# Inverting three head pairs beside the first scan of a RWKV-7 / Mamba-2 / MoE block instead of one

## The chip, the cores and the metric

The kernel runs on one core of a Trainium2 chip. The metric is device time in microseconds of one execution; lower is better. A core has five engines with a queue each: TensorE (PE in the rows; PEld is its weight load), VectorE (DVE), ScalarE (ACT), GpSimd (POOL) and SyncE (SP), whose queue here issues most of the transfers.

## What is computed

The reference is one layer of a backbone: a mixer of two parallel branches (bidirectional RWKV-7 and bidirectional Mamba-2), merged by gates, and then a mixture of experts, over 512 latent and 256 context tokens of width 1024. The change lies in the RWKV-7 branch, whose core is this recurrence, run forwards and backwards for 16 heads of 64:

```python
def step(s, inp):
    r_t, w_t, k_t, v_t, kk_t, a_t = inp
    sa = jnp.einsum('bhvk,bhk->bhv', s, -kk_t)
    s = s * w_t[:, :, None, :] + sa[..., None] * (kk_t * a_t)[:, :, None, :] + v_t[..., None] * k_t[:, :, None, :]
    return s, jnp.einsum('bhvk,bhk->bhv', s, r_t)
```

## The kernel before

**The chunked form.** The kernel cuts the 768 tokens into 12 chunks of 64 and works on pairs of heads, 0 to 7. Within a chunk the recurrence is a triangular system, so each chunk needs the inverse of a 64x64 unit triangular matrix. With 12 chunks, two heads and two directions, that is 48 matrices for each pair.

**The preparation.** `rw_all` goes through the eight pairs. For each it makes the decay products (`rw_elem`) and the masked products of a chunk (`rw_products`), once for each direction, and stores them in HBM: the 32x32 diagonal blocks go to `d1`, the off-diagonal block to `d3`. After the second direction it runs the pair's inverse, `tri`.

**The inverse, first step.** `tri` (L768 to L810) loads the blocks of `d1` into `Ad` with three transfers, works out the inverses of the 32x32 blocks on VectorE (L783 to L805), turns them on ScalarE (L808) and stores them and their transposes in `d2`. It is a generator with 16 resumptions: eight in the loop of L783 and L784, four in that of L795 and L797, four in that of L803 and L805. All pairs share the tiles `T` and `Tf`, so the inverses run one after the other.

**The inverse, second step.** `tri2` (L812 to L853) loads two pieces from `d2` and `d3` with eight transfers, waits `LAG` resumptions (if called with the tag "A"), multiplies them on TensorE in four groups of 48 small matmuls (`px`, L835, and `py`, L845) with a copy by ScalarE after each, and stores the full 64x64 inverses in `TTd` for the scan. It has `LAG` + 5 resumptions with that tag. In the preparation the second step of pairs 0 to 4 runs two pairs later, within `rw_products`.

**The scan.** `scan` does the 12 chunk steps of two pairs at once, so there are four scans. A step has three hand-overs on TensorE: `pr` (the right side, L901) is copied to `R` by VectorE (L929); `pq` = inverse times `R` is copied into `SV`, half by VectorE (L943) and half by ScalarE (L944); `pn`, the new state, is multiplied by the decay on VectorE (L953). Between the hand-overs `feed(HOP)`, with `HOP` = 3200, puts columns of the input projection (L311, L314) on TensorE: the filler, 24 blocks with a convolution behind each on VectorE and ScalarE (L464, L467), together with two late parts of the modulation, which it draws in between. The filler has about as many columns as the four scans ask for. A block needs its weights split in two (`whi` L283 on ScalarE, `wlo` L286 on VectorE).

**The side work.** Scan 0 also resumes a generator five times in each step (once after `R`, once after `pq`, three times, `SS`, at the end), 60 times in all; it is `rw_last`, with `LAG` = 9. It lets four resumptions pass, then runs the second step of pair 5, the first step of pair 7, and the second steps of pairs 6 and 7. What is left of it runs after scan 0, with `feed(SF)` after each resumption and `SF` = 2000. Scan 1 needs none of the results of pairs 5 to 7; scan 2 needs pair 5's, scan 3 those of pairs 6 and 7. After scan 3 the readout of the last two pairs (`rw_out`) runs alone, and the gate projections and the SSD stage follow.

**What sets the order.** In these stages only TensorE keeps the written order (`manual_schedule(engines={PE})`). The queues of VectorE, ScalarE, GpSimd and SyncE are put in order ahead of time by a planner, which works with costs of its own and prefers what was written earlier among the operations that are ready.

Of the kernel before, what the change touches and what calls it, by code (L numbers as in the profile page):

```python
# [35 lines left out]
ORB = 1  # L36
N1 = 15000
N2 = 11000
LAG = 9
R0 = 3000  # L40
SF = 2000
HE = 0, 1
SS = 3
RA = 0
PL = (0, 1, -1, -2, 2, 3, 4, 5, 6, 7)
PO = (0, 1, 2, 3, 4, 5, 6, 7, 8, 9)
FH = 2
# [39 lines left out]
class Block:  # L87
# [468 lines left out]
    def rw_all(self, pool, ps, z):  # L556

        self.fill, self.credit = self.rw_in(pool, z), 0
        next(self.fill)
        hop = R0  # L560
        f = lambda x=1: self.feed(x * (hop if len(self.kvr) < 8 else RHT))
        self.pair = {}
        self.drain(0)
        self.rw_head(pool, ps, 0, f)
        op = self.rw_elem(pool, ps, 0, 0, f)
        t2 = iter(())
        for p in range(8):
            nxt = self.rw_elem(pool, ps, p, 1, f)
            hop = RHOP
            self.rw_products(pool, ps, p, 0, *op, f, t2)  # L570
            op = nxt
            if 1 < p < 7:
                t2 = self.tri2(self.tp, ps, "ra", p - 2)
                next(t2)
            if p < 7:
                self.drain(p + 1)
            self.rw_bonus(pool, ps, p)
            if p < 7:
                self.rw_head(pool, ps, p + 1, f)
                nxt = self.rw_elem(pool, ps, p + 1, 0, f)  # L580
            self.rw_products(pool, ps, p, 1, *op, f, t2, p == 7)
            op = nxt
            if p < 7:
                self.finish(self.tri(self.tp, p))
        self.feed(1 << 30)

    def rw_last(self, ps):

        for _ in range(4):
            yield  # L590
        yield from self.tri2(self.tp, ps, "A", 5)
        yield from self.tri(self.tp, 7)
        yield from self.tri2(self.tp, ps, "A", 6)
        yield from self.tri2(self.tp, ps, "A", 7)

    def two(self, ps):
        return ps.tile([128, SEQ], F32, name="ra", tag="ra"), ps.tile([128, CTX], F32, name="rac", tag="ra")
# [214 lines left out]
    def tri2(self, pool, ps, tag, p):  # L812
# [12 lines left out]
        for d in range(2):  # L825
            nc.sync.dma_start(A21[64 * d:64 * d + 32], d3[d])
        for _ in range(LAG if tag == "A" else 1):
            yield
# [65 lines left out]
    def scan(self, pool, ps, p, side):  # L894
# [10 lines left out]
        for s in range(12):  # L905
# [19 lines left out]
            R = pool.tile([128, 2, 2, 64], F32, name="R", tag="R", bufs=2)  # L925
            if p == 0 and s < RA:
                nc.scalar.activation(R, pr, AF.Copy)
# [1026 lines left out]
def body(tc, A, out):  # L1954
    with ExitStack() as ctx:
# [28 lines left out]
        with ExitStack() as hx:  # L1984
# [22 lines left out]
            with pl("ip", space=PSUM) as B.ip, pl("sc") as sc, pl("scp", space=PSUM) as scp, ExitStack() as scx:  # L2007
# [5 lines left out]
                with tc.manual_schedule(engines={mybir.EngineType.PE}):  # L2013
                    for p in range(4):
                        py = B.scan(sc, scp, p, side)
                        if p == 0:
                            for _ in side:
                                B.feed(SF)
                            tpx.close()
# [96 lines left out]
```

## Time and profile before

| | us |
|---|---|
| median of three runs | 2141.14 |
| lowest and highest | 2135.18, 2143.14 |
| profiled execution, its own time | 2138.47 |
| its span, first to last instruction | 2136.7 |
| mean granted TensorE clock (share of full speed) | 0.933 |

The profile records one execution. The preparation runs until about 623 us, scan 0 from there to about 758, the scans 1 to 3 to about 1102. A row of a timeline gives the start, the duration, the engine and the line, what was written from what, and how often; in square brackets stands the time for which the engine idled before it, if any, and what released it. `pch` is the psum tile of all three hand-overs of a scan, so its rows are told apart by their inputs: `SV,sAL` makes the right side, `R,sTT` the value, `SV,sBT` the new state. In the first two steps the inputs have other names (`sAR`, `sBK`), as they lie in buffers of the preparation.

### The profile page before, as it was taken

The numbers are of one execution on the slowest core, as the hardware profiler recorded it, in microseconds if no ns is written. First come the engines' busy times: TensorE is split into PE (matmuls) and PEld (weight loads), VectorE is DVE, ScalarE is ACT, GpSimd is POOL, SyncE is SP. The second block draws the span as 40 slices with busy tenths as digits, with TensorE's granted clock in tenths as the row PEclk, the third lists the DMA queues.
The fourth block names the chain that finished last, engine by engine and source line by source line (L and its number), as shares of the span: only waits on it lengthen the run. The fifth ranks groups of instructions, "written<-read, shape, count | busy, mean of one in ns | idle before, by whom it ended". The sixth has DMA issues, their size and how long they took to land.

```text
span 2136.7 us, 34532 instructions
## 1 busy us (share of the span) xinstructions
PE 1880.0 (88%) x13683; PEld 1255.7 (59%) x13696; DVE 1244.5 (58%) x2234; ACT 840.0 (39%) x1344; POOL 259.2 (12%) x383
## 2 busy tenths in 40 slices
PE   5978898888869988999998997799999999999997
PEld 2867676676646756667675664377877453433332
DVE  4466988897888567555654898864364022322224
ACT  5454565545624343443543453353233131111113
POOL 1123323133220000000000000000001000000002
PEclk8999989999979989999998998889999999999998
DMA  6357687777888766785536353358567989999997
GB/s 239 89 128 179 161 201 181 177 175 184 206 199 241 229 225 217 257 254 157 180 102 203 121 170 104 108 180 287 187 247 292 355 333 362 409 409 409 409 409 292
DMA packets 388414, 495.13 MB, mean 232 GB/s; under 512 B 138521, under 2 KB 278031, under 8 KB 385179
## 3 DMA queue, kind: packets, MB, share of 16 engines
q1 hardware_dynamic: 349883, 407.33, 57.4%
q0 software_dynamic: 21504, 68.70, 11.0%
q10 hardware_dynamic: 16864, 16.88, 2.5%
q8 instruction: 108, 1.77, 0.3%
q14 instruction: 55, 0.45, 0.1%
HBM read 393.96 MB, written 97.98 MB: 230 GB/s over the span
## 4 chain that ended last, share of the span: by engine, by line
PE 53%; DVE 18%; DMA 13%; ACT 8%; issue 6%; POOL 1%; SPq 1%; ACTq 0%; POOLq 0%; DVEq 0%
PE ph L1712 9%; PE pl L311 9%; DMA wraw<-in_w_in_dram 5%; PE pye L1799 5%; PE pch L901 4%; PE mp L1361 4%; PE pc L314 3%; DVE wlo L286 2%; DMA ew<-in_exp_w_dram 2%; PE psc L1822 1%; PE sps L1180 1%; ACT whi L283 1%; PE py L901 1%; PE pl L1314 1%; PE adaps L167 1%
## 5 line engine op out<-in xcount | busy, mean ns | idle before, releaser
L311 PE MATMUL pl<-hlH,whi 128*128 128x512 f32 x672 | 244.1, 443 | 14.2 <-ACT u L455 5.6
L311 PE MATMUL pl<-hlH,wlo 128*128 128x512 f32 x672 | 236.3, 428 | 0.0
L311 PE MATMUL pl<-hlL,whi 128*128 128x512 f32 x672 | 231.9, 425 | 0.0
L1713 PE MATMUL ph<-ew,xe 128*64 128x512 f32 x432 | 196.3, 597 | 2.1 <-DMA ew<-in_exp_w_dram 2.1
L1712 PE MATMUL ph<-ew,xe 128*64 128x512 f32 x432 | 196.0, 596 | 0.0
L283 ACT ACTIVATE whi<-wraw 128x1024 fp32r<-128x1024 f32 x93 | 97.8, 1052 | 182.2 <-DMA wraw<-in_w_in_dram 79.1
L311 PEld LDWEIGHTS pl<-hlH,whi 128*128 128x128 f32 x672 | 132.8, 202 | 56.7 <-issue 14.1
L286 DVE TENSOR_TENSOR wlo<-wraw,whi 128x1024 fp32r<-128x1024 f32 x93 | 112.8, 1212 | 84.1 <-ACT whi L283 58.7
L311 PEld LDWEIGHTS pl<-hlL,whi 128*128 128x128 f32 x672 | 129.3, 196 | 38.1 <-issue 11.4
L311 PEld LDWEIGHTS pl<-hlH,wlo 128*128 128x128 f32 x672 | 128.3, 196 | 36.6 <-issue 12.6
L1712 PEld LDWEIGHTS ph<-ew,xe 128*64 128x64 f32 x432 | 56.3, 137 | 105.9 <-issue 104.5
L1799 PE MATMUL pye<-ew,ewx 128*64 128x512 f32 x448 | 108.3, 635 | 0.0
L314 PE MATMUL pc<-hcH,whi 128*128 128x256 f32 (+1 forms) x312 | 97.2, 315 | 7.1 <-ACT u L455 6.1
L464 DVE SCALAR_TENSOR_TENSOR cacc<-u,cst,cacc 128x772 f32<-128x772 f32 (+1 forms) x96 | 93.3, 972 | 11.1 <-ACT cacc L460 9.6
L314 PE MATMUL pc<-hcL,whi 128*128 128x256 f32 (+1 forms) x312 | 94.6, 307 | 0.0
L314 PE MATMUL pc<-hcH,wlo 128*128 128x256 f32 (+1 forms) x312 | 94.4, 304 | 0.0
L1719 ACT ACTIVATE ewx<-ph 128x512 f32<-128x512 f32 x30 | 17.9, 598 | 187.2 <-PE ph L1713 170.0
L1827 DVE TENSOR_TENSOR macc<-macc,psc 128x512 f32<-128x512 f32 x56 | 37.7, 685 | 91.4 <-PE psc L1822 91.3
L314 PEld LDWEIGHTS pc<-hcH,whi 128*128 128x128 f32 (+1 forms) x312 | 63.0, 202 | 15.8 <-ACT u L455 9.2
L1799 PEld LDWEIGHTS pye<-ew,ewx 128*64 128x64 f32 x448 | 32.7, 146 | 63.8 <-issue 63.1
L1815 DVE TENSOR_TENSOR yhl<-yf,yhl 64x512 fp32r<-64x512 f32 x30 | 20.5, 686 | 81.0 <-ACT yhl L1814 80.5
L1217 ACT ACTIVATE X<-selb,ncumT 128x128 f32<-128x128 f32 x128 | 36.4, 367 | 78.4 <-PE selb L1214 78.3
(594 smaller groups left out, 4100.4 us busy)
## 6 DMA issues: line engine op xcount, KB each, us to landing
ew<-in_exp_w_dram SPq DMA_DIRECT2D x126, 1024.0 KB
ew<-in_exp_w_dram SPq DMA_DIRECT2D x90, 512.0 KB
wraw<-in_w_in_dram SPq DMA_DIRECT2D x83, 512.0 KB
adaw<-in_ada_w_dram SPq DMA_DIRECT2D x24, 1024.0 KB
cst<-in_exp_w_dram SPq DMA_DIRECT2D x14, 1024.0 KB
BTd<-BT ACTq DMA_DIRECT2D x48, 256.0 KB
sAL<-ALd SPq DMA_DIRECT2D x23, 512.0 KB
sBT<-BTd SPq DMA_DIRECT2D x23, 512.0 KB
```

The costliest lines, as they stand in the source:

```text
L283: pin(nc.scalar.activation(hi, raw, AF.Copy))
L286: self.lo.tensor_sub(lo, raw, hi.bitcast(F32))
L311: nc.tensor.matmul(pl[:n], w_[:, kt, :n], x[0][:, kt, :], **e)
L314: nc.tensor.matmul(pc[:n], w_[:, kt, :n], x[1][:, kt, :], **e)
L464: e.scalar_tensor_tensor(acc[:, s0:s0 + n0], u[:, s0 + k:s0 + k + n0], cw[:, b, k:k + 1], acc[:, s0:s0 + n0], op0=OP.mult, op1=OP.add)
L901: mm = lambda o, w, x, f=True, l=True: nc.tensor.matmul(o, w, x, start=f, stop=l, skip_group_check=True)
L1217: nc.scalar.activation(X[:, c], pt[d][:, c], AF.Identity, bias=self.ncumT[:, c, r:r + 1])
L1361: nc.tensor.matmul(po[ob], w[k][lo][:, ob * 128:ob * 128 + 128], yb[k][:, h], start=k + h + lo == 0, stop=k == 15 and lo == 1)
L1712: nc.tensor.matmul(ph[e][f][0:64], x, w1[j][:, fs], start=kt == 0, stop=kt == 7, skip_group_check=True)
L1713: nc.tensor.matmul(ph[e][f][64:128], x, w3[j][:, fs], start=kt == 0, stop=kt == 7, skip_group_check=True)
L1799: nc.tensor.matmul(py[64 * c:64 * c + 64], hd[e][:, kt], w2[j][:, 512 * c:512 * c + 512], start=kt == 0, stop=kt == 7, skip_group_check=True)
L1827: nc.vector.tensor_add(a, a, pc)
```

## The change

The preparation now runs `tri` only for pairs 0 to 4. The side work of scan 0 begins with `tri` of pair 5, then runs `tri` of pair 6 and `tri2` of pair 5 by turns, then `tri` of pair 7 and `tri2` of pair 6 by turns, then `tri2` of pair 7. A new helper, `both`, resumes its generators in turn. `LAG` goes from 9 to 4, `SF` from 2000 to 3000, and `RA` from 0 to 2: in the first two steps of scan 0, `R` is copied by ScalarE (the branch was there already, and was never taken with `RA` = 0).

```diff
-LAG = 9
+LAG = 4
 R0 = 3000
-SF = 2000
+SF = 3000
 HE = 0, 1
 SS = 3
-RA = 0
+RA = 2
...
             op = nxt
-            if p < 7:
+            if p < 5:
                 self.finish(self.tri(self.tp, p))
         self.feed(1 << 30)
 
     def rw_last(self, ps):
 
-        for _ in range(4):
-            yield
-        yield from self.tri2(self.tp, ps, "A", 5)
-        yield from self.tri(self.tp, 7)
-        yield from self.tri2(self.tp, ps, "A", 6)
+        yield from self.tri(self.tp, 5)
+        yield from self.both(self.tri(self.tp, 6), self.tri2(self.tp, ps, "A", 5))
+        yield from self.both(self.tri(self.tp, 7), self.tri2(self.tp, ps, "A", 6))
         yield from self.tri2(self.tp, ps, "A", 7)
+
+    def both(self, *gens):
+
+        gens = list(gens)
+        while gens:
+            for g in list(gens):
+                try:
+                    next(g)
+                except StopIteration:
+                    gens.remove(g)
+                    continue
+                yield
```

## Rows read from the trace of the kernel before

**Rows 1.** Page, busy time, share of the span and instructions of each engine.

```profile
PE 1880.0 (88%) x13683; PEld 1255.7 (59%) x13696; DVE 1244.5 (58%) x2234; ACT 840.0 (39%) x1344; POOL 259.2 (12%) x383
```

**Rows 2.** Windows: length, busy (count) of PE, PEld, DVE, ACT, POOL; PE clock, DMA, GB/s.

```profile
580.00:600.00 20.00, 13.58 (x112) 9.65 (x111) 17.94 (x34) 10.68 (x18) 10.69 (x13) 0.95 0.79 177
600.00:623.00 23.00, 18.50 (x105) 12.71 (x107) 15.90 (x45) 4.83 (x6) 2.00 (x4) 0.67 0.69 185
623.00:640.00 17.00, 8.18 (x73) 6.26 (x73) 16.48 (x38) 2.83 (x6) 3.98 (x6) 0.70 1.06 231
740.00:757.00 17.00, 14.85 (x272) 12.52 (x273) 6.67 (x14) 5.75 (x11) 1.31 (x3) 0.74 0.63 195
987.00:1102.00 115.00, 107.48 (x1185) 81.36 (x1185) 68.32 (x102) 51.59 (x69) 7.46 (x14) 0.96 0.46 143
...
623.00:758.50 135.50, 117.69 (x1741) 92.73 (x1741) 93.82 (x198) 52.44 (x79) 10.76 (x20) 0.90 0.81 228
```

**Rows 3.** Windows for the inverses' VectorE operations alone: length, their busy time (count).

```profile
582.00:600.00 18.00, 5.28 (x15) 0.94 0.74 165
612.00:645.00 33.00, 24.62 (x72) 0.69 0.90 209
623.00:758.50 135.50, 40.69 (x107) 0.90 0.81 228
```

**Rows 4.** Timeline of TensorE, end of the preparation and start of scan 0.

```profile
600.18 2.04 PE L713 MATMUL pb<-ksum,cst 128*128 128x512 f32 x2 [3.67 <-DVE ksum L711]
...
634.86 1.12 PE L901 MATMUL pch<-R,sBK 64*64 64x64 f32 x16 [8.82 <-DVE R L929]
...
643.92 0.68 PE L901 MATMUL pch<-R,sBK 64*64 64x64 f32 x16
```

**Rows 5.** Timeline of VectorE, the same stretch.

```profile
599.30 0.74 DVE L711 SCALAR_TENSOR_TENSOR ksum<-ksum,cst,r 128x512 f32<-128x512 f32 x1
...
634.45 0.36 DVE L929 COPY R<-pch 128x256 f32<-128x256 f32 x1
...
642.50 0.42 DVE L929 COPY R<-pch 128x256 f32<-128x256 f32 x1
...
645.02 0.14 DVE L783 TENSOR_TENSOR pr<-T,Ad 96x2 f32<-96x2 f32 x1
...
654.38 1.00 DVE L464 SCALAR_TENSOR_TENSOR cacc<-u,cst,cacc 128x772 f32<-128x772 f32 x1
```

**Rows 6.** Timeline of ScalarE (ACTq issues its transfers), the same stretch.

```profile
628.31 4.20 ACTq L763 DMA_DIRECT2D BTd<-BT  x2
632.56 0.60 ACT L483 ACTIVATE zg<-pl 128x512 f32<-128x512 f32 x1 [11.09 <-DMA BTd<-BT]
...
650.23 0.43 ACT L454 ACTIVATE u<-pc 128x256 f32<-128x256 f32 x1
```

**Rows 7.** Timeline of the sync queue, the same stretch.

```profile
622.56 3.20 SPq L821 DMA_DIRECT2D TT<-d  x4
```

**Rows 8.** Timeline of TensorE, pair 7's second step and scan 1's first products.

```profile
746.92 0.95 PE L835 MATMUL px<-T,A 32*32 32x32 f32 x48 [1.08 <-ACT A L838]
748.95 1.49 PE L845 MATMUL py<-TT,A 32*32 32x32 f32 x48 [1.08 <-ACT A L838]
...
758.53 0.69 PE L901 MATMUL pch<-SV,sAL 128*64 128x64 f32 x16
```

**Rows 9.** Timeline of TensorE in scan 3: two projection pitches, two step starts.

```profile
1067.01 0.40 PE L311 MATMUL pl<-hlL,whi 128*128 128x512 f32 x1
...
1067.36 0.40 PE L311 MATMUL pl<-hlL,whi 128*128 128x512 f32 x1
...
1070.40 0.69 PE L901 MATMUL pch<-SV,sAL 128*64 128x64 f32 x16
...
1078.47 0.69 PE L901 MATMUL pch<-SV,sAL 128*64 128x64 f32 x16
```

**Rows 10.** Timeline of TensorE, the readout behind scan 3.

```profile
1122.52 1.12 PE L980 MATMUL po<-oy,cst 128*128 128x512 f32 x2 [2.15 <-DVE od L996]
```

## The prediction, made blind

> **What bounds the kernel now.** I read the page's busy table first [rows 1]: TensorE is busy for 1880 of 2136.7 us and no other engine for more than 58%. So time can be won only where TensorE stands still or runs slowly. The windows give the places near the change [rows 2]. From 580 to 640 us, which is the end of the preparation stage and the start of scan 0, TensorE is busy for 13.58 of 20, 18.50 of 23 and 8.18 of 17 us, at a granted clock of 0.95, 0.67 and 0.70; the last scan, 987 to 1102, has 107.48 of 115 us at 0.96. Here 1.00 would be the full 2.4 GHz and 0.5 the 1.2 GHz level, so a mean of 0.67 means that the engine spent about two thirds of the stretch at the lower level.
>
> The timelines say why. The inverse of one pair is a chain of 62 small VectorE operations; they take 21 to 22 us (24.62 us in 612 to 645, less about 3 us that end the pair before) [rows 3]. VectorE is full from 582 to 600, with 5.28 us of such operations among its 17.94 [rows 3], and the bonus multiply that TensorE needs comes at 599.30 [rows 5], so TensorE waits 3.67 us [rows 4]. At the first step of scan 0 it waits 8.82 us for the copy R [rows 4]: the copy ran only at 634.45 [rows 5], behind much of pair 6's inverse in VectorE's queue. After that the same 16 matmuls take 1.12 us, against 0.68 us one step later [rows 4]; that is what the lower level costs.
>
> **The change, part by part.** Only TensorE keeps the written order. The other queues are planned ahead, and what is written later gets a later claim: pair 7's inverse is written into steps 4 to 7 of scan 0, yet begins at 645.02, in step 2 [rows 5]. So "moved into the scan" means that pairs 5 and 6 now give way to the preparation of pairs 6 and 7, and fill its gaps; it does not mean that all 44 us go behind the scan's start.
>
> (a) End of preparation. Of the 5.28 us of inverse operations between the multiplies at 582 to 600, most stand ahead of the work that TensorE waits for. All gone would be -6.4 us, all that TensorE idles from 580 to 600 (20 - 13.58) [rows 2]; nothing gone would be 0. I take -5, since VectorE had next to no free time there.
>
> (b) First right side. Two R copies go to ScalarE; the nearest form, a 128x256 copy from PSUM by ScalarE, takes 0.43 us [rows 6], as long as VectorE's 0.42 [rows 5]. So the operation costs nothing and its place is all. ScalarE's queue, however, is itself held: it issues two stores at 628.31 and its next operation starts at 632.56 after 11.09 us of idling on one of them [rows 6]. If R stands behind that, it runs at about 633 and nothing is won; if it stands ahead, all 8.82 us go. Ahead of ScalarE's stores the sync queue issued the loads of pair 5's second step, the last four from 622.56 to 625.8 [rows 7]; these belong to a pair that is now written later. I take -8, nearer the full end.
>
> (c) The clock. 600 to 640 holds 26.7 us of TensorE work at about 0.68 [rows 2]. By the pair 1.12 and 0.68 us [rows 4] a stretch at the lower level costs 1.65 times its time, so the bounds are 0 and about -8; I take -4, as the waits of (a) and (b) go only in part.
>
> (d) VectorE within scan 0. From 623 to 758.5 VectorE is busy for 93.82 us, 40.69 of them inverses [rows 2, 3]. Three whole inverses are 66 us, so at most 25 us come in, against 41.7 us free. The chain's copies then wait more often for the operation ahead of them; with 36 hand-overs in the scan I put +2, between 0 and +13 (22 us / 62 = 0.35 us, one inverse operation, at each).
>
> (e) Queues passed. Each moved pair brings three loads of its factors, two stores, eight loads of its second step and two stores again, all on the sync queue, and on ScalarE four copies, one of them the turning of the finished inverse. They now stand behind the scan's loads for the next steps. I put this at 0: the scan's loads no longer wait behind them; should the cover fail, the second step of pair 5 is late. It is needed only in step 5 instead of step 2, some 25 us later, and a late load of it would be at most the 3 us or so that its issue takes [rows 7].
>
> (f) Pair 7's second step. Now its four groups on TensorE stand bare: waits of 1.08 us and 1.49 us for 48 matmuls [rows 8]. Afterwards 3000 columns stand between any two resumptions, 1.4 us of work, which covers 1.08 us. I take -2, between 0 and -3.5.
>
> (g) Columns moved. A resumption count settles it. Before, the side work has 4+14+16+14+14 = 62 resumptions, the twelve steps make 60, and 2 remain with 2000 columns each. Afterwards it has 16+25+25+9 = 75, of which 15 remain with 3000: 45,000 columns, 41,000 more than before. A pair of matmuls of 512 and 256 columns takes 0.35 us [rows 9], so 18.7 us of projection move from the end of scan 3 to the gap after scan 0. The amounts cancel. But scan 3 then runs its last 41,000/9,600 = 4.3 steps with no projection between its hand-overs. A step takes 8.07 us now [rows 9], of which 4.4 are columns; some 1.4 us per step (the two halves of the value copy, one after the other, at about R's 0.42 us each [rows 5] and the gaps between, and the state multiply past what covers it) come to light, so +6. Against that the last convolution is over earlier, and the readout behind scan 3, which now stands still by itself (2.15 us at 1122.52) [rows 10], meets a freer VectorE and ScalarE: -2. I take +4, between 0 and +16.
>
> What the rows show on the clock at this place: the bare groups of pair 7's second step ran in a stretch granted 0.74, while scan 3, with columns in every gap, had 0.96 [rows 2]. If a bare step's own matmuls, 8.07 - 4.4 = 3.7 us, ran at the lower level, it would be 3.7 x 0.65 x 4.3 = +10 more, and the sum below would be -3 in place of -13. The Trainium skill (TensorE: Matmul & The Clock Gate, What's actually happening) says that being throttled is the default and that activity releases it, which speaks against taking dense columns out of scan 3; by that rule the sum is the -3, and the trace's 0.74 agrees with it as far as it goes.
>
> **Sum:** -5 - 8 - 4 + 2 - 2 + 4 = -13 us. The profiled execution took 2138.47 us (span 2136.7 and 1.8 around it), 2.7 below the median of the three runs, 2141.14. On the median that is 2128.
>
> **The rivals.** *Nothing moves that counts.* The planner already put inverses wherever VectorE was free, and ScalarE holds R behind the stores at 632.56 [rows 6]. Then (b) and (c) are nothing, (a) gives -5, and (d) with (g) take about +6: 2142, no change. For it speaks the 11.09 us; against it that the loads ahead of those stores belong to the moved pair. Chance 0.26.
>
> *Scan 3 ends at the lower level.* The start is won, but the 4.3 bare steps run at 1.2 GHz and give 10 us back: -3, 2138, no change to be measured. For it speaks the 0.74 [rows 2]; against it that the pauses of a bare step, about 1 us, are shorter than the 8.82 us that stood before the slow stretch at 634.86 [rows 4]. Chance 0.10.
>
> *VectorE becomes the bound of scan 0.* Three inverses are written ahead of the chain's value copy and state multiply, and only R leaves that queue. If they are queued as R was in the kernel before, the 8.82 us moves from R to the next value copy, (b) and (c) are lost, and the scan stretches: inverses 66, other VectorE work 93.82 - 40.69 = 53, and 14 for the convolutions of the columns drawn forward (2.2 blocks of 18,432 columns, each with some six operations of about the 1.00 us of a tap [rows 5]) make 133 us in a stretch in which TensorE has some 136. Two engines so alike in load, each waiting for the other, add about +15; with (a) -5 and (g) +4 that is +14: 2155, slower. It decides when the inverses run past scan 0, so that the remaining 15 resumptions wait for pair 7. For it speaks R's wait; against it that the first operation of each inverse has so far started as soon as the last one ended, ahead of where it was written, and that the steps under pair 7's inverse were scarcely longer than others. Chance 0.18.
>
> *The forecast* keeps 0.46. Half a per cent, 10.7 us, is about what a measurement of this kernel can tell from no change; the forecast's own range is 2112 to 2132, and a little of it falls within half a per cent. I give 0.44 faster, 0.38 no change, 0.18 slower. The range 2110 to 2150 holds the forecast, the two rivals without a change and the milder part of the slower one.
>
> **What would show it.** Right: TensorE's wait for R in scan 0's first step is under 3 us and R runs on ScalarE; the granted clock over the first steps is near 1.0; scan 1 begins only a few microseconds later than 758.53 [rows 8] although 18.7 us of columns have moved ahead of it; scan 3's last four or so steps take 5 to 6 us, not 8.07; VectorE is over 85% busy in scan 0. Wrong: ScalarE idles on a store up to R; TensorE waits in the gap after scan 0 for pair 7's second step, with VectorE still at its inverse; or the bare steps of scan 3 run at a clock below 0.8.

## The result, and the profile after

**2152.81 us**, the median of 4 runs (2151.25 to 2153.53), beside 2140.44 us (2135.18 to 2143.14) for four runs of the kernel before: ratio 1.0057, 95% interval 1.0031 to 1.0082. The change is slower by 12.4 us, a little over the half per cent; the forecast was 13 us faster, and the time lies above its range.

The profiled execution took 2153.53 us. The page's span and busy table [rows 1] show no engine with as much as 1 us more to do:

```profile
span 2151.8 us, 34515 instructions
PE 1874.5 (87%) x13683; PEld 1252.3 (58%) x13696; DVE 1244.2 (58%) x2232; ACT 840.7 (39%) x1345; POOL 259.3 (12%) x383
```

So the 15.1 us between the two spans are waiting. The starts of the same matmuls in both traces say where:

| stretch on TensorE | before | after | difference |
|---|---|---|---|
| start to scan 0's first products | 622.94 | 626.45 | +3.5 |
| scan 0, to the products with R of its last step | 118.96 | 129.76 | +10.8 |
| from there to scan 1's first products (the gap) | 16.63 | 31.82 | +15.2 |
| scans 1 to 3 and the readout, to the SSD stage | 384.37 | 367.70 | -16.7 |
| the rest | 993.8 | 996.1 | +2.3 |

The first line is not read as a cost: with only `SF` changed (run 9 below), so that the preparation is the same, scan 0 began at 627.66 in place of 622.94. Stretches from scan 0's start are compared below. There the change is +9.3 us, over the three lines in the middle. From here on the steps of a scan are counted from 0.

Windows of the changed kernel answer to [rows 2] (columns as there); the last two rows are scan 0 with the gap, and what follows up to the SSD stage:

```profile
580.00:600.00 20.00, 17.81 (x124) 13.26 (x122) 16.66 (x33) 8.96 (x15) 7.83 (x9) 0.87 0.76 172
600.00:626.00 26.00, 16.98 (x109) 11.85 (x110) 18.71 (x41) 4.91 (x6) 4.36 (x7) 0.80 0.69 188
626.00:642.00 16.00, 4.09 (x40) 2.69 (x40) 15.10 (x43) 4.93 (x10) 4.50 (x7) 0.72 0.93 236
626.45:788.03 161.58, 135.26 (x1839) 107.60 (x1839) 109.44 (x216) 65.05 (x96) 12.43 (x23) 0.90 0.75 208
788.03:1155.73 367.70, 321.03 (x3517) 224.78 (x3520) 214.49 (x335) 152.94 (x199) 23.48 (x45) 0.94 0.65 209
```

From 580 to 600 TensorE idles 2.2 us, no longer 6.4; from 600 to 626 it idles 9.0, where it had 4.5 in 600 to 623. What the one place won, the next lost. The inverses did not leave: VectorE spends 5.58 us on them from 582 to 600, where it had 5.28, and 19.84 us from 612 to 645, where it had 24.62 [rows 3]:

```profile
582.00:600.00 18.00, 5.58 (x15) 0.91 0.75 170
612.00:645.00 33.00, 19.84 (x58) 0.72 0.75 191
```

On VectorE's timeline the first operations of the inverses of pairs 5, 6 and 7 start at

```profile
558.64 0.15 DVE L793 TENSOR_TENSOR pr<-T,Ad 96x2 f32<-96x2 f32 x1
...
624.20 0.15 DVE L793 TENSOR_TENSOR pr<-T,Ad 96x2 f32<-96x2 f32 x1
...
652.21 0.14 DVE L793 TENSOR_TENSOR pr<-T,Ad 96x2 f32<-96x2 f32 x1
```

against 645.02 before for pair 7 [rows 5], and for pairs 5 and 6

```profile
554.72 0.14 DVE L783 TENSOR_TENSOR pr<-T,Ad 96x2 f32<-96x2 f32 x1
...
616.79 0.15 DVE L783 TENSOR_TENSOR pr<-T,Ad 96x2 f32<-96x2 f32 x1
```

So pairs 5 and 6, written a stage later, run 4 and 7 us later; pair 7, which was in scan 0 already, runs 7 us later too.

TensorE's timeline in scan 0 answers to [rows 4] (code behind the diff stands 10 lines further down):

```profile
641.53 1.12 PE L911 MATMUL pch<-R,sBK 64*64 64x64 f32 x16 [11.25 <-ACT R L937]
...
674.49 1.12 PE L911 MATMUL pch<-R,sTT 64*64 64x64 f32 x16 [8.04 <-DVE R L939]
...
706.52 0.68 PE L911 MATMUL pch<-R,sTT 64*64 64x64 f32 x16 [1.41 <-DVE R L939]
...
780.70 0.95 PE L855 MATMUL py<-TT,A 32*32 32x32 f32 x48 [0.48 <-ACT A L848]
```

The wait for R in step 0 is 11.25 us instead of 8.82, a wait of 8.04 us in step 3 is new, and pair 7's second step in the gap now waits 0.48 us once. ScalarE's timeline names what R stood behind in step 0, and what happened before step 3:

```profile
639.97 0.64 ACT L799 ACTIVATE Tt<-T 96x256 f32<-96x256 f32 x1 [2.84 <-DVE pr L805]
640.51 0.40 ACT L800 ACTIVATE Tf<-T 96x256 f32<-96x256 f32 x1
640.82 0.40 ACT L801 ACTIVATE Tf<-T 96x256 f32<-96x256 f32 x1
641.12 0.36 ACT L937 ACTIVATE R<-pch 128x256 f32<-128x256 f32 x1
...
669.77 1.06 ACT L283 ACTIVATE whi<-wraw 128x1024 fp32r<-128x1024 f32 x1 [8.98 <-DMA wraw<-in_w_in_dram]
670.84 1.28 ACT L466 ACT_TABLE_LOAD   x1
672.13 0.85 ACT L466 ACTIVATE csg<-cacc 128x772 f32<-128x772 f32 x1
```

R on ScalarE ran right behind the three copies of pair 6's inverse. In step 3 the chain has five links: a load of weights, asked for at 659.64, is there only at 669.77; `whi`, which rounds it, blocks ScalarE for 8.98 us; behind `whi` stands the sigmoid `csg` of an earlier convolution; its product is what VectorE waits for; and R is next in VectorE's queue:

```profile
673.01 0.96 DVE L467 TENSOR_TENSOR cacc<-cacc,csg 128x772 f32<-128x772 f32 x1 [8.59 <-ACT csg L466]
674.01 0.42 DVE L939 COPY R<-pch 128x256 f32<-128x256 f32 x1
```

In the kernel before that load takes as long (asked for at 652.20, used at 662.53), but the two ScalarE operations stand the other way round, between copies of pair 5's second step:

```profile
656.52 0.98 ACT L838 ACTIVATE A<-px 32x384 f32<-32x384 f32 x2 [1.66 <-PE px L835]
657.51 1.28 ACT L466 ACT_TABLE_LOAD   x1
658.81 0.85 ACT L466 ACTIVATE csg<-cacc 128x772 f32<-128x772 f32 x1
659.68 0.98 ACT L838 ACTIVATE A<-px 32x384 f32<-32x384 f32 x2
662.53 1.06 ACT L283 ACTIVATE whi<-wraw 128x1024 fp32r<-128x1024 f32 x1 [1.87 <-DMA wraw<-in_w_in_dram]
```

### The profile page after: what moved, and what is told of

It reads as the page before. It is cut to its first block, busy times and chain, and to the rows that moved or that the text cites. A ratio compares the mean times of both kernels' runs of the same rounds, so it can differ in the third digit from the quotient of the medians.

```text
span 2151.8 us, 34515 instructions
## 1 busy us (share of the span) xinstructions
PE 1874.5 (87%) x13683; PEld 1252.3 (58%) x13696; DVE 1244.2 (58%) x2232; ACT 840.7 (39%) x1345; POOL 259.3 (12%) x383
## 4 chain that ended last, share of the span: by engine, by line
PE 40%; DVE 7%; DMA 5%; ACT 4%; issue 2%; SPq 0%; POOL 0%; POOLq 0%; DVEq 0%; ACTq 0%
PE ph L1722 8%; PE pye L1809 5%; PE pl L311 5%; PE mp L1371 4%; DMA ew<-in_exp_w_dram 2%; PE pch L911 2%; PE pl L1324 2%; PE psc L1832 1%; PE pc L314 1%; PE sps L1190 1%; PE rp L1682 1%; PE warm L1550 1%; PE rp L1683 1%; PE wo L1424 1%; PE wo L1422 1%
## 5 line engine op out<-in xcount | busy, mean ns | idle before, releaser
L464 DVE SCALAR_TENSOR_TENSOR cacc<-u,cst,cacc 128x772 f32<-128x772 f32 (+1 forms) x96 | 93.4, 973 | 12.5 <-ACT cacc L460 10.8
```

The lines of the kernel that those rows point to most:

```text
L464: e.scalar_tensor_tensor(acc[:, s0:s0 + n0], u[:, s0 + k:s0 + k + n0], cw[:, b, k:k + 1], acc[:, s0:s0 + n0], op0=OP.mult, op1=OP.add)
```

## The experiments

Three theories at first. **A**: the loss is places in queues; the moved work has put something in front of R. **B**: it is the 41,000 columns drawn forward. **C**: VectorE has no room in scan 0 for three inverses. After the first four runs A was split: **S**, the swapped pair (`whi` ahead of `csg`) makes the wait of step 3; **H**, pair 6's inverse makes that of step 0. Each ratio is to runs of the kernel before on the same chip. A table of all runs stands at the end of the section.

**1. R back on VectorE** (in the changed kernel):

```diff
-RA = 2
+RA = 0
```

> The changed kernel with RA = 0: both R copies back on VectorE, all else as changed. Theory A (the places in the queues: the planner leaves the inverses where they were, and R only changes the queue in which it stands behind pair 6's inverse): TensorE's first wait for R is 8 to 10 us instead of 11.25, the wait of 8.04 us at step 3 stays, and the time is 2148 to 2152. Theory B (the loss comes from the 41,000 columns drawn forward): no difference that can be told, 2151 to 2155.

Ratio 1.0061 (1.0044 to 1.0078), as with the change. R of step 0 waits 10.59 us, now in VectorE's queue, behind pair 6's inverse itself; step 3 waits 7.14. Theory A comes near on the waits, but the time, 2156.29 us, is above its range: which engine copies R decides nothing.

**2. Few columns behind scan 0** (changed kernel):

```diff
-SF = 3000
+SF = 270
```

> The changed kernel with SF = 270, so that the 15 resumptions behind scan 0 draw some 4,000 columns, as in the kernel before, and not 45,000. Theory A: scan 0 keeps its waits (11.25 and 8.04 us); the columns go back to scan 3's end, which wins 2 us at most, and pair 7's second step stands bare again: 2150 to 2156. Theory B: the time falls back to 2139 to 2144.

Ratio 1.0040 (1.0024 to 1.0056): lower by 0.17%, 3.6 us, with intervals that overlap. Both waits for R stay, 11.54 and 6.95 us. B is not the main cause.

**3. R on ScalarE in the kernel before.**

```diff
-RA = 0
+RA = 2
```

> The kernel before with RA = 2 alone. Theory A: R stands behind pair 6's copies in ScalarE's queue, as it stood behind its operations in VectorE's; TensorE's first wait for R is 9 to 12 us instead of 8.82, and the time is 2140 to 2145. The prediction's view (ScalarE frees R): the wait is under 3 us and the time 2130 to 2134.

Ratio 0.9998 (0.9985 to 1.0011). R waits 8.75 us on ScalarE, where it waited 8.82 on VectorE: on ScalarE it stands behind the stores `BTd` and the same three copies. This is the prediction's largest term measured by itself: nothing.

**4. VectorE held to the written order in scan 0** (changed kernel, `RA` = 0):

```diff
-                        py = B.scan(sc, scp, p, side)
+                        if p == 0:
+                            with tc.manual_schedule(engines={mybir.EngineType.PE, mybir.EngineType.DVE}):
+                                py = B.scan(sc, scp, p, side)
+                        else:
+                            py = B.scan(sc, scp, p, side)
```

> The changed kernel with RA = 0 and VectorE held to the written order in scan 0, as TensorE is, so that the inverses of pairs 5 to 7 can't run ahead of where they are written. Theory A: R of step 0 stands ahead of all three inverses, its wait is under 3 us, the end of the preparation has no inverse of pair 5 or 6 left and is 3 to 6 us shorter, the clock over the first steps is above 0.9; the time is 2136 to 2146. Theory C (VectorE has no room for three inverses beside scan 0, wherever they stand): the chain's copies wait behind them, scan 0 and the gap behind it take over 170 us instead of 161.6, and the time is 2152 to 2165.

Ratio 1.0295 (1.0277 to 1.0313), the slowest of all. Step 0's wait for R is gone, but TensorE waits at many later steps (8.98, 6.82, 5.98 and 5.84 us are the longest for VectorE), and scan 0 with the gap takes 215.59 us at a granted clock of 0.80. Holding the whole queue is no remedy; the later runs hold single operations. C's mark, over 170 us, is passed without C's cause: VectorE is busy for 137.69 of those 215.59 us. And the run shows what the end of the preparation would win if the inverses did leave it: here none of their operations runs from 570 us to scan 0, and from pair 4's second step to scan 0's first products it takes 50.07 us, where run 1 takes 55.74.

**5. The sigmoid first.** In the changed kernel, `whi` of that one block is queued behind `csg`; nothing else:

```diff
+            if i == 2 and k[0] == "c":
+                with self.tc.issue_after(self.sig):
+                    wn = load(*blocks[i + 1])
...
-        nc.scalar.activation(sg[:, s:s + n], acc[:, s:s + n], AF.Sigmoid)
+        sig = nc.scalar.activation(sg[:, s:s + n], acc[:, s:s + n], AF.Sigmoid).ins
+        if b == 16:
+            self.sig = sig
```

> The changed kernel with one pair of instructions on ScalarE in the other order: the rounding of the weights of block 4 (whi) is queued behind the sigmoid of block 1 (csg), as it was before the change. Nothing else is held. Theory S (the swapped pair): in the changed kernel the copy R of step 3 waits 8.04 us behind the convolution's last product, this behind the sigmoid, this behind whi, and whi for its weights, which were asked for at 659.64 and used at 669.77; with the sigmoid first the wait at step 3 falls below 1.5 us and the time by 6 to 8 us, to about 2146, ratio to before 1.001 to 1.003. Theory C (VectorE has no room for three inverses): the same 8 us come up at a later R or in the gap behind scan 0; time and ratio stay, 2153 and 1.005 to 1.006.

Ratio 1.0031 (1.0018 to 1.0045): 0.26% or 5.6 us less than the change, in intervals that overlap, and just short of what was expected. On ScalarE's timeline the sigmoid no longer waits for the weights:

```profile
664.60 0.85 ACT L466 ACTIVATE csg<-cacc 128x772 f32<-128x772 f32 x1 [0.35 <-DVE cacc L464]
671.08 1.06 ACT L283 ACTIVATE whi<-wraw 128x1024 fp32r<-128x1024 f32 x1 [5.63 <-DMA wraw<-in_w_in_dram]
```

and on TensorE's R of step 3 comes without a wait:

```profile
668.54 0.68 PE L917 MATMUL pch<-R,sTT 64*64 64x64 f32 x16
674.04 1.23 PE L917 MATMUL pch<-SV,sBT 128*64 128x64 f32 x10 [3.10 <-DVE SV L959]
```

Of the 8 us, 3.1 come back at the next hand-over, where VectorE's half of the value copy is late.

**6. R first.** Changed kernel, `RA` = 0; what pairs 6 and 7 put on VectorE is queued behind R of step 0 (`self.r0`):

```diff
+    def behind(self, gen):
+        while True:
+            with self.tc.issue_after(self.r0):
+                try:
+                    next(gen)
+                except StopIteration:
+                    return
+            yield
...
-        yield from self.both(self.tri(self.tp, 6), self.tri2(self.tp, ps, "A", 5))
-        yield from self.both(self.tri(self.tp, 7), self.tri2(self.tp, ps, "A", 6))
+        yield from self.behind(self.both(self.tri(self.tp, 6), self.tri2(self.tp, ps, "A", 5)))
+        yield from self.behind(self.both(self.tri(self.tp, 7), self.tri2(self.tp, ps, "A", 6)))
```

> The changed kernel with R of steps 0 and 1 on VectorE, and with what pairs 6 and 7 put on VectorE queued behind R of step 0. Theory H (R of step 0 is late because pair 6's inverse stands ahead of it): the 10.6 us that TensorE waits in step 0 fall below 3 us, and the time by 7 to 9 us against the 2156 of the changed kernel with R on VectorE, to about 2148; step 3 still waits its 7 us. Theory C: pair 6's inverse, now begun some 15 us later, ends later too, pair 7's second step is waited for in the gap behind scan 0, and no more than 3 us are won; 2153 to 2160.

Ratio 1.0049 (1.0031 to 1.0066). H holds for the wait: step 0's is gone altogether. It does not hold for the time: 0.12% against run 1, inside the intervals. In step 3, where the swap is still there, the wait has passed from R to the value copy (6.04 us).

**7. Both:** run 6, and `whi` behind the sigmoid in two blocks (the edit of run 5, with `i in (2, 3)`).

> As the run with R first, and the weights' rounding queued behind the sigmoid of the block before in two blocks. Theories S and H together: the waits of steps 0 and 3 are both gone, some 15 us against the changed kernel with R on VectorE, 2138 to 2142, at or a little below the kernel before (ratio 0.996 to 1.000). Theory C: 2150 or more; the waits come up at later steps.

Ratio 1.0044 (1.0030 to 1.0059), where 0.996 to 1.000 was expected. TensorE's timeline has no wait for R left, and others in their place, at the value and the new right side of the first steps:

```profile
633.33 1.11 PE L927 MATMUL pch<-sAR 128*64 128x64 f32 x14 [4.08 <-ACT sAR L972]
...
649.10 1.00 PE L927 MATMUL pch<-SV,sAL 128*64 128x64 f32 x16 [3.45 <-DMA sAL<-ALd]
```

The first is ScalarE's half of the value copy, behind the stores of the last BT factors; the second the scan's own load of its next factors.

**8. The cause alone.** In the kernel before, the side work begins one scan step later, with pair 5's second step (`SF` keeps the columns equal). What follows it is written later too, but pair 7's inverse, the only one there, still starts 22.07 us behind the scan's first products (22.08 before):

```diff
-SF = 2000
+SF = 570
...
-        for _ in range(4):
+        for _ in range(9):
             yield
         yield from self.tri2(self.tp, ps, "A", 5)
```

> The kernel before with one edit: pair 5's second step is written five resumptions later (9 for 4), one scan step; the columns fed behind the scan are kept at 4000 in all. All inverses stay where they were. Theory S: what keeps whi behind the sigmoid in the kernel before is only that pair 5's second step holds ScalarE's queue between them; with it gone the wait of 7 to 8 us at step 3 appears, R of step 0 waits 8.8 us as before, and the time rises by 5 to 8 us, to about 2147, ratio 1.002 to 1.004. Theory C: with no inverse moved nothing changes; 2141, ratio 1.000.

Ratio 1.0033 (1.0022 to 1.0045), +6.5 us: as theory S expected. The wait appears in the kernel before, on TensorE's timeline:

```profile
672.93 1.12 PE L901 MATMUL pch<-R,sTT 64*64 64x64 f32 x16 [5.67 <-DVE R L929]
```

and ScalarE's has the same swap:

```profile
667.94 1.06 ACT L283 ACTIVATE whi<-wraw 128x1024 fp32r<-128x1024 f32 x1 [6.37 <-DMA wraw<-in_w_in_dram]
669.01 1.28 ACT L466 ACT_TABLE_LOAD   x1
670.31 0.85 ACT L466 ACTIVATE csg<-cacc 128x772 f32<-128x772 f32 x1
```

**9. The columns alone**, in the kernel before:

```diff
-SF = 2000
+SF = 22500
```

> The kernel before with one number changed: the two resumptions behind scan 0 are fed 22,500 columns each, not 2000, so that the same 41,000 columns leave the end of scan 3 as in the change; nothing else. Theory S with columns as a smaller second cost: what leaves scan 3 isn't all won back; the stretch from scan 0 to scan 1 grows by 18 to 19 us and that from scan 1 to the next stage shrinks by 14 to 18, the time rises by 1 to 4 us, to 2142 to 2145, ratio 1.000 to 1.002. Theory B (the columns are the main loss): 2150 or more, ratio over 1.004.

Ratio 1.0030 (1.0014 to 1.0045), 8.1 us: between the two theories. From scan 1 to the SSD stage 18.6 us are won back, all that moved; but the gap grew by 22.9 us. Here the columns come in one piece behind pair 7's second step, and TensorE waits for a convolution's input copy in front of a new block:

```profile
782.03 0.58 PE L314 MATMUL pc<-hcH,whi 128*128 128x256 f32 x1 [3.47 <-ACT u L455]
```

In the change they lie between the groups of the second step, at a clock of 1.00, and the gap costs less than the columns. So this run overprices the change's columns; run 2 prices them at 3.6 us.

**10. Runs 2 and 5 together** (`SF` = 270 and the sigmoid first, in the changed kernel).

> The changed kernel with the sigmoid of block 1 ahead of the rounding of block 4's weights and only 4050 columns fed behind scan 0, as the kernel before does it. If the swapped pair and the columns are two separate costs, their sum goes: of the change's 0.57% some 0.26 and 0.17 leave, ratio 1.000 to 1.003, time about 2144. If they are one cost seen twice, it stays at 1.003 or more.

Ratio 1.0025 (1.0012 to 1.0039), inside the expected range but at its upper end: 0.32% of 0.57% are gone, less than 0.26 + 0.17. Step 0 waits 12.22 us here, and with few columns pair 7's second step waits 2.57 us for a load.

**11. All repaired:** run 7 with `SF` = 270 and both halves of step 0's value copy on VectorE.

```diff
+            if p == 0 and s == 0:
+                nc.vector.tensor_copy(SV[H[1], :, 1, j], pq[H[1]])
+            else:
+                nc.scalar.activation(SV[H[1], :, 1, j], pq[H[1]], AF.Copy)
```

> The changed kernel with R of steps 0 and 1 on VectorE, VectorE's work for pairs 6 and 7 queued behind R of step 0, the sigmoids ahead of the rounding of weights in two blocks, 4050 columns behind scan 0, and in step 0 both halves of the value copy on VectorE (in the run that had R first, TensorE waited 4.08 us for the half on ScalarE, which stood behind stores). If the change loses only by places in queues, the waits of steps 0 and 3 are both gone and the time falls below the kernel before: 2132 to 2138, ratio 0.996 to 0.999. If late loads on the sync queue take over (3.45 us for sAL in the run with both), 2140 to 2146.

Ratio 1.0053 (1.0032 to 1.0074); even the worse case was missed. The half copy that was moved is no longer late, but that of step 1 is (4.40 us), then `sAL` (2.99), then ScalarE's half in step 3 (3.09).

**12. R first in the kernel before:** pair 6's inverse alone is written behind R of step 0 and queued behind it, and step 0's value copy is VectorE's, as in run 11.

```diff
-            if p < 7:
+            if p < 6:
                 self.finish(self.tri(self.tp, p))
...
+        with self.tc.issue_after(self.r0):
+            self.finish(self.tri(self.tp, 6))
         for _ in range(4):
             yield
```

> The kernel before, with one inverse moved by 62 VectorE operations and no more: pair 6's, written behind R of step 0 and queued behind it, and step 0's value copy with both halves on VectorE. Pair 5's second step stays where it was, so the sigmoid stays ahead of the weights' rounding. Expected: the 8.82 us of step 0 fall below 2 us and step 3 does not wait; 6 to 9 us won, 2131 to 2135, ratio 0.996 to 0.997. If another load or store takes the place of R, as the run with R first showed in part, no more than 3 us are won: 2138 to 2141.

Ratio 1.0010 (0.9996 to 1.0024): 8.82 us of waiting removed from the kernel before, and nothing won. Up to R of step 3 the scan is 3.3 us shorter (39.51 for 42.80), and from there to scan 1 it is 9.0 us longer (101.81 for 92.79), with VectorE busy for 69.45 us in place of 55.92, as pair 6's inverse is now there. In the first part TensorE's next wait is for the scan's first BT factors, those of the new state:

```profile
641.87 1.12 PE L903 MATMUL pch<-sAR 128*64 128x64 f32 x16 [6.73 <-DMA sAR<-BTd]
```

and on the sync queue's timeline that load stands behind six loads of pair 5's second step, the last four of which took 5.89 us to issue (3.20 in [rows 7]):

```profile
631.24 5.89 SPq L823 DMA_DIRECT2D TT<-d  x4
637.44 0.38 SPq L888 DMA_DIRECT2D sAR<-BTd  x1
```

**13. R and the scan's loads first:** run 12, with pair 5's second step queued behind that BT load on the sync queue, and the loads of pair 6's inverse behind those of the scan's second group.

```diff
+        with self.tc.issue_after(self.r0), self.tc.issue_after(self.bt):
+            self.finish(self.tri(self.tp, 6))
...
+        five = self.tri2(self.tp, ps, "A", 5)
+        with self.tc.issue_after(self.bt0):
+            next(five)
```

> The run that put R first in the kernel before, with two more places changed on the sync queue: the loads of pair 5's second step are queued behind the load of the scan's first BT factors, and the loads of pair 6's inverse behind those of the scan's second group. There R's 8.82 us had gone and 6.73 us for that BT load (issued at 637.44, behind six loads of pair 5) and 1.68 us for sAL had come. Theory L (R's wait lay over late loads of the scan's own factors): with the loads first, these two waits fall below 2 us together, the scan's first three steps take some 8 us less than in the kernel before, and the time falls to 2133 to 2138, ratio 0.995 to 0.998. Rival T (the loads and stores of the end of the preparation keep the transfer engines full, so that whatever comes last waits): the BT load lands no earlier than about 8 us behind the scan's start, or another load takes its place; ratio 0.999 to 1.002.

Ratio 1.0027 (1.0012 to 1.0043). The two waits went, and a longer one came, 19.73 us for R of step 1. VectorE's timeline shows why:

```profile
630.39 0.88 DVE L966 TENSOR_TENSOR sAR<-pch,cst 64x256 f32<-64x256 f32 x2 [1.29 <-PE pch L907]
652.60 0.16 DVE L789 TENSOR_TENSOR pr<-T,Ad 96x2 f32<-96x2 f32 x1 [21.33 <-DMA Ad<-d]
...
654.00 0.42 DVE L937 COPY R<-pch 128x256 f32<-128x256 f32 x1
```

The first operation of pair 6's inverse had been queued ahead of that R, and VectorE stood idle for 21.33 us until its load, now one of the last, had landed. During that wait, from 640 to 660, TensorE was busy for 5.52 of 20 us and granted 0.55.

**14. The change with all loads of the scan first:** run 11 with `SF` = 3000, both halves of the copy on VectorE in steps 0 and 1, and the loads of pairs 5 (second step), 6 and 7 behind those of the scan's second group.

```diff
-            with self.tc.issue_after(self.r0):
+            with self.tc.issue_after(self.r0), self.tc.issue_after(self.bt1):
```

> The changed kernel with its 3000 columns, R of steps 0 and 1 and both halves of the value copy of steps 0 and 1 on VectorE, VectorE's work of pairs 6 and 7 behind R of step 0, their loads and pair 5's second step's behind the loads of the scan's second group, and the sigmoids of two blocks ahead of the rounding of weights. Theory L: the waits of 4.4 us (half copy behind stores) and 3.0 us (sAL) of the run with all repaired are gone, and the change stands at or below the kernel before: 2136 to 2142, ratio 0.997 to 1.000. Rival T: other waits take their place, ratio 1.003 or more.

Ratio 1.0048 (1.0031 to 1.0066). R of step 2 waits 11.26 us, again on VectorE. Both runs speak against L (the scan's own loads first), and a wait for another load came as T has it (run 13's ratio lies above T's range too). Why that load was late they do not settle: the edit itself had put it behind the scan's loads, and its three transfers took 7.04 us to issue in run 13 and 6.87 in run 14.

All runs together. Waits for R and lengths are from each kernel's profiled execution; "idle" is a stretch's length less TensorE's busy time in the windows, up to the products with R of step 3, from there to scan 1, and from there to the SSD stage; "length" is all three. One execution can lie far from its kernel's median (run 12's took 2156.23 us, the median of its 12 is 2144.75), so a few microseconds between two lengths tell nothing by themselves.

| kernel | ratio | R, step 0 | R, step 3 | idle, three stretches | length |
|---|---|---|---|---|---|
| before | 1 | 8.82 | 0 | 10.9, 6.9, 40.6 | 520.0 |
| 3 R on ScalarE | 0.9998 | 8.75 | 0 | 11.1, 6.0, 44.1 | 521.8 |
| 8 second step later | 1.0033 | 8.81 | 5.67 | 15.4, 6.1, 42.3 | 525.9 |
| 9 columns | 1.0030 | 8.83 | 0.44 | 11.0, 11.3, 43.1 | 525.6 |
| 12 R first | 1.0010 | 0 | 0 | 9.5, 11.0, 42.4 | 526.7 |
| 13 and loads | 1.0027 | 0 | 0 | 20.9, 10.8, 41.3 | 531.4 |
| change | 1.0057 | 11.25 | 8.04 | 20.0, 6.3, 46.7 | 529.3 |
| 1 R on VectorE | 1.0061 | 10.59 | 7.14 | 19.1, 9.3, 47.6 | 533.6 |
| 2 few columns | 1.0040 | 11.54 | 6.95 | 18.8, 9.9, 40.2 | 528.9 |
| 4 VectorE held | 1.0295 | 0 | 2.13 | 21.0, 37.0, 50.6 | 589.8 |
| 5 sigmoid first | 1.0031 | 10.65 | 0 | 10.7, 9.5, 47.6 | 527.9 |
| 10 two and five | 1.0025 | 12.22 | 0 | 12.2, 12.8, 39.4 | 526.2 |
| 6 R first | 1.0049 | 0 | 0 | 7.8, 15.6, 46.8 | 527.2 |
| 7 both | 1.0044 | 0 | 0 | 8.5, 13.4, 47.8 | 528.8 |
| 11 all repaired | 1.0053 | 0 | 0 | 9.3, 17.7, 40.5 | 530.9 |
| 14 and loads | 1.0048 | 0 | 0 | 13.5, 13.3, 48.4 | 532.3 |

What to see in it: the swap idles TensorE in the first stretch, by 4.5 us in run 8 against before and 9.3 in the change against run 5. Where R comes first, the second stretch idles 4 to 8 us more (run 12 against before, 6 and 7 against 1, 11 against 2), with VectorE's work of the inverses pushed into it. Changed kernels with 3000 columns per resumption idle 6 to 9 us more in the third than those with 270. No kernel here beats the one before.

## Why the prediction was wrong

Point by point, by the steps' letters.

- **(a), end of the preparation, -5: wrong in what moves, not in its price.** The stretch from pair 4's second step to scan 0's first products went from 58.44 to 56.70 us, -1.7. The step argued that pairs 5 and 6 would "give way"; their operations ran within 4 to 7 us of where they had run. That is what the rival "nothing moves that counts" said. Where they did go, in run 4, the stretch was 5.7 us shorter than in run 1.
- **(b), R on ScalarE, -8: the step that failed most.** The choice went to "nearer the full end" because the loads ahead of ScalarE's stores belong to a pair written later. Those loads did go (`TT<-d` is issued from 636.94 on), but R was still behind the stores and behind pair 6's three copies, and waited 2.4 us longer; the prediction had named the stores, but not the copies. Two more things were missing. First, run 3 prices the engine at nothing. Second, even the whole wait was not to be had: run 12 takes it out of the kernel before and wins nothing. The scan's first BT load (6.73 us) and its next factors (1.68 us) come right behind, and pair 6's inverse, now behind R, lengthens the later steps (by 9.0 us in the profiled execution). The prediction never asked what would be late next behind this wait.
- **(c), the clock, -4: nothing.** It hung on (a) and (b): the matmuls behind R still take 1.12 us, and up to step 1 of the scan the granted clock is 0.69 (626.45 to 648.21), where it was 0.72 (622.94 to 641.06).
- **(d), VectorE within scan 0, +2 between 0 and +13:** R's waits behind step 0 add 9.4 us, inside the bounds, but the mechanism was another one. VectorE was not the bound (109.44 busy of 161.58 us); it stood idle for 8.59 us, waiting for a sigmoid. So it is luck that the rival with VectorE as the bound, at 2155, came nearest to 2152.81: its sign, inverses that run past scan 0, did not come, as the last one ended at about 708 us.
- **(e), queues passed, 0: wrong, and the largest single loss.** The cover named for it, that pair 5's second step isn't needed for 25 us, held. What the step left out is what the moved work had been doing where it stood: its copies on ScalarE ran between the sigmoid and the rounding of weights. With them gone, the rounding came first and held ScalarE until its load landed. The step counted four copies on ScalarE for each pair, those of `tri`; the eight of its second step, the very ones that left, are not in its list. Undone in the change this is worth 5.6 us (run 5), done alone in the kernel before it costs 6.5 (run 8).
- **(f), pair 7's second step, -2: right,** and a little small. Scan 0's gap went from 16.63 to 31.82 us; less the 18.7 us of columns this is -3.5, the end of its range. Little of it is waiting (TensorE idles 1.3 us there, it was 2.1); the granted clock in the gap went from 0.69 to 1.00.
- **(g), columns moved, +4: about right in price, not in what was laid bare.** The last stretch won back 16.7 of 18.7 us, so +2.0; it is between +2 and +5.5 in the other changed kernels with the same columns and +0.1 in run 9. Run 2 prices (f) and (g) together at +3.6 us, in intervals that overlap. The sum 41,000/9,600 = 4.3 steps took the columns to end with scan 3. In the kernel before they ran on for some 18 us behind it, between the products of the readout, and most of what moved came from there. So only the last two steps of scan 3 lost all their columns (they start at 1116.48 and 1121.02, 4.54 us apart), and the readout lost them too. First the kernel before, behind scan 3; then the change, with the end of scan 3 (its first 4 us still have columns) and the readout:

```profile
1101.60:1120.40 18.80, 17.68 (x78) 13.23 (x75) 8.89 (x9) 12.22 (x15) 2.06 (x4) 1.00 0.28 85
...
1109.00:1123.00 14.00, 11.62 (x221) 8.87 (x221) 4.94 (x10) 1.82 (x3) 0.00 (x0) 1.00 0.32 88
1125.00:1149.00 24.00, 11.50 (x12) 2.80 (x12) 6.70 (x10) 13.37 (x17) 0.54 (x1) 0.56 0.52 178
```

  The lower level that was feared for the bare steps came in the readout instead, at a granted clock of 0.56: its six pairs of products take 11.5 us together, where they took 8.3 (before, only the last two pairs ran at that level, 2.07 us each). The Trainium skill (TensorE: Matmul & The Clock Gate, What's actually happening) says that the throttled state is the default and activity releases it. By the sum that followed from it the 4.3 steps would have cost 10 us more; the two that were bare did not lose the clock (1.00 from 1116.48 to 1125, too). In the bare readout, and behind run 13's wait of 19.73 us (0.55), it did fall, and there the trace agrees.

From scan 0's start the parts are: +2.4 (step 0), +8.0 (step 3) and +1.4 (step 6) of waits for R, -3.5 in the gap and +2.0 behind it. That makes +10.3, where the stretch shows +9.3. Run 5 prices the wait in step 3 at 5.6 us, less than its 8.0.

**What stays open.** With the swap undone and few columns, 0.25% are left (run 10), some 5 us. Its waits suggest step 0 (12.22 against 8.82 us), the value copy of step 3 (3.01 us) and the load that pair 7's second step waits for in the gap; none was tried alone. Why the start of the scan can't be hurried is shown only in part. Runs 6, 7, 11, 12, 13 and 14 each remove the wait for R in step 0 and each get another wait within the first four steps: a half copy behind stores, the BT load, `sAL`, or an inverse's operation with its load outstanding. In all of them the transfer engines are full in these steps: over the first 27 us of scan 0 the DMA share is 0.96 to 1.03 in these six and 0.97 in the change. In the kernel before the window from 623 to 650 has

```profile
623.00:650.00 27.00, 17.39 (x165) 13.15 (x166) 24.57 (x66) 7.04 (x10) 3.98 (x6) 0.81 1.06 244
```

with a DMA share of 1.06. The Trainium skill (DMA: Bandwidth & Descriptors, Issuing engines are not separate DMA queues) says that transfers of all issuing engines run on the same 16 engines and interleave; by that a better place on one queue makes no room. The shares agree with it. That the amount of data, and not the order of the loads, is the floor is argued, not shown: no run took transfers away.

## What to carry to other kernels

Where queues are ordered by a planner, writing work later in the program need not move it late in time (here by 4 to 7 us); look up when it ran before, and whether anything else wanted that slot. Price a moved step by what it stood between, not only by what it does: here a few copies on ScalarE kept a sigmoid ahead of an operation that waits for a load, and their leaving made up about half of the loss (5.6 of 12.4 us by run 5). Before a wait is counted as a gain, find the second latest input of the same instruction and of the next two steps, in the trace or by one run that takes the first away.

## What the runs showed of the hardware that was not expected

The time to issue the same transfers is not fixed: the four loads `TT<-d` took 3.20 us to issue in the kernel before and 5.89 in run 12, and all that stands behind them on the sync queue is late by as much. The load of the transfer engines does not tell the two apart (a DMA share of 0.98 from 622.5 to 626 and of 0.96 from 631 to 638); the cause stays open. And one operation with an outstanding load stops its whole queue: 0.16 us of work held VectorE for 21.33 us in run 13, with the copy TensorE needed two steps behind it.
